# Squared key lengths from the diagonal of the key scores, on VectorE, in a gated delta rule

## The chip, the cores and the metric

One core of a Trainium2 chip runs the whole program in one launch. The time is device microseconds of one execution; the profiled execution also has a trace of every instruction.

## The reference

One layer of a hybrid block on 256 tokens of width 2048, batch 1, all in float32. A modulated RMSNorm of `x` goes through one wide input projection. Its columns feed two branches: a bidirectional mLSTM (4 heads) and a bidirectional gated delta rule (16 heads of width 128). Both are projected back, merged by gates and projected once more; a SwiGLU feed-forward part (5632 wide) and a last RMSNorm follow. The change is inside the gated delta rule, in the lengths of keys and queries:

```python
def l2_normalize(a):
    return a * lax.rsqrt(jnp.sum(a * a, axis=-1, keepdims=True) + EPS)

q_b = l2_normalize(heads(b_q, B_HEADS, B_DK)) * (B_DK ** -0.5)
k_b = l2_normalize(heads(b_k, B_HEADS, B_DK))
...
a_mat = jnp.eye(CHUNK) + betac[..., :, None] * jnp.einsum('nbhid,nbhjd->nbhij', kc, kc) * decay_strict
t_mat = lax.linalg.triangular_solve(a_mat, eye, left_side=True, lower=True, unit_diagonal=True)
u = jnp.einsum('nbhij,nbhje->nbhie', t_mat, betac[..., None] * vc)
```

For each token and head one needs the squared length of its key and of its query. The products of all keys with all keys, which the rule needs anyway, hold the squared key lengths on their diagonal.

## The kernel before

Large products run on TensorE in a split form: a float32 weight tile is copied to a high part `wh` by ScalarE (lines 178 and 209), VectorE subtracts it to get the low part `wl` (lines 180 and 211), and three matmuls a tile (lines 183 to 185, or 230 to 232) give the product. `wh` and `wl` have three buffers each. The jobs that do this (`fjob`, `tjob`) are generators; they are the filler between the steps of the delta rule, and `pump` adds a row product of the modulation (line 123, on VectorE) from time to time.

The delta rule runs head by head through `gdn_phase1`. Step one of a head makes the decay masks `dec` by scans on VectorE, splits keys and queries `kq` (128 x 2 x 256, width by kind by token) into `kqh` and `kql`, squares `kq` on ScalarE (`sqkq`, line 602), transposes the values into the PSUM tile `vps` (line 605), and multiplies each of the four 128-token blocks of squares by a column of ones (line 607). These four one-column products leave the squared lengths of keys and queries in columns 256 to 259 of `vps`, one token to a partition. Step two takes their roots (line 615, Sqrt on ScalarE), the reciprocals `r4`, the squared reciprocal of the key length, and from it and `beta` the factors `sig` and `nsg` (lines 616 to 622, four small VectorE instructions), and scales the values into `vv` (line 625, ScalarE, which frees `vps`). Then for each of the two 128-token blocks `t` three matmuls give the scores `ks` of its keys with all keys and queries (lines 636 to 638), and VectorE makes five masked products of them: `mi` and `mb` from the diagonal block (lines 643 and 644, with `nsg` as a factor for each partition), `gg` and `at` from the rest (lines 646 to 652). A 32x32 transpose (line 653) fills the second half of `mi`, GpSimd's queue stores blocks of it (`inst_d`, line 659), and ScalarE copies corners of `mi` and `mb` to `cc`.

After four heads, `gdn_invert` solves the small triangles on VectorE, and `gdn_phase2` runs two heads at a time through short products (`p`, `pa`, `pb`, `pc`, `po`, `px`) while `stream` feeds in the projections (`b_job`, a convolution and Silu on the way) and `gdn_phase1` of the heads of the next group. `vps`, `ks` and all tiles of the second phase come from one PSUM pool of four banks, `g_ps`.

The order of instructions on an engine is not the order of the text: a planner lists them by simulated readiness, with the text's order as priority, and only instructions wrapped in `order(...)` stay behind their predecessor on that engine. None of the lines that the change touches is wrapped.

Of the kernel before, what the change touches and what calls it, by code (L numbers as in the profile page):

```python
# [9 lines left out]
F32 = mybir.dt.float32  # L10
F32R = mybir.dt.float32r
AF = mybir.ActivationFunctionType
# [3 lines left out]
P = 128  # L16
T = 256
# [35 lines left out]
def hybrid_block(ctx: ExitStack, tc: tile.TileContext, xr, nfr, crow, pk_d, cst_d, ada2, ada4, win0, winb, wint, wba, wbb, wo, wgu, wd, out, dbg=None):  # L53
# [529 lines left out]
    def gdn_phase1(h):  # L583
# [16 lines left out]
        V.tensor_tensor(kl, kq, kh.bitcast(F32), ALU.subtract)  # L600
        sq = fr.tile([P, 2, T], F32, tag="sqkq", bufs=1, name=f"sqkq{h}")
        S.activation(sq, kq, AF.Square)
        vps = gps(f"vps{h}")
        for t in range(2):
            PE.transpose(vps[:, t * P : (t + 1) * P], vf[:, t * P : (t + 1) * P], ident)
        for c in range(4):
            PE.matmul(
                vps[:, 256 + c : 257 + c], sq[:, c // 2, (c % 2) * P : (c % 2 + 1) * P], ones1, start=True, stop=True
            )
        yield  # L610
# [3 lines left out]
        nn = fr.tile([P, 8], F32, tag="nn", bufs=2, name=f"nn{h}")  # L614
        S.activation(nn[:, 0:4], vps[:, 256:260], AF.Sqrt, bias=epsc)
        V.reciprocal(r4, nn[:, 0:4])
        V.tensor_tensor(nn[:, 4:6], r4[:, 0:2], r4[:, 0:2], ALU.mult)
        beta = bT[:, :, h::16]
        sg3, ns3 = (a.rearrange("p (t d) -> p t d", t=2) for a in (sig, nsg))
        rk2 = nn[:, 4:6].unsqueeze(2).broadcast_to([P, 2, 2])  # L620
        V.tensor_tensor(sg3, beta, rk2, ALU.mult)
        V.tensor_scalar(nsg, sig, -1.0, None, ALU.mult)
        vv = bk.tile([P, 2, P], F32, tag="vv", bufs=NB, name=f"vv{h}")
        for t in range(2):
            S.activation(vv[:, t], vps[:, t * P : (t + 1) * P], AF.Copy, scale=nn[:, t : t + 1])


# [3 lines left out]
        at = bk.tile([P, 2, 384], F32, tag="at", bufs=NB, name=f"at{h}")  # L631
        for t in range(2):
            ks = gps(f"ks{h}_{t}")
            c = slice(t * P, (t + 1) * P)
            mh, ml_ = (a.rearrange("p j t -> p t j") for a in (kh, kl))
            PE.matmul(ks, kh[:, 0, c], mh, start=True, stop=False)
            PE.matmul(ks, kh[:, 0, c], ml_, start=False, stop=False)
            PE.matmul(ks, kl[:, 0, c], mh, start=False, stop=True)
            kk, qk = (a for a in (ks.rearrange("p (t j) -> p j t", j=2)[:, j] for j in range(2)))
            dg = kk[:, t * P : (t + 1) * P]  # L640
            fdiag = dec[:, 0, 0:P] if t == 0 else dec[:, 0, 256:384]
            bdiag = dec[:, 1, 256:384] if t == 0 else dec[:, 1, P:256]
            V.scalar_tensor_tensor(mi[:, t], dg, ns3[:, t, 0:1], fdiag, ALU.mult, ALU.mult)
            V.scalar_tensor_tensor(mb[:, t], dg, ns3[:, t, 1:2], bdiag, ALU.mult, ALU.mult)
            if t == 0:
                V.tensor_tensor(gg[:, 0], kk[:, P:], dec[:, 0, P:256], ALU.mult)
                V.tensor_tensor(at[:, 0, 0:256], qk, dec[:, 0, 0:256], ALU.mult)
                V.tensor_tensor(at[:, 1, 256:384], qk[:, 0:P], dec[:, 1, 256:384], ALU.mult)
            else:
                V.tensor_tensor(gg[:, 1], kk[:, 0:P], dec[:, 1, 0:P], ALU.mult)  # L650
                V.tensor_tensor(at[:, 0, 256:384], qk[:, P:], dec[:, 0, 256:384], ALU.mult)
                V.tensor_tensor(at[:, 1, 0:256], qk, dec[:, 1, 0:256], ALU.mult)
        V.transpose(mi[:, 2:4].rearrange("p t c -> p (t c)"), mb.rearrange("p t c -> p (t c)"))
        g, hl_ = divmod(h, GRP)
# [902 lines left out]
```

## Time and profile before

| | us |
|---|---|
| Runs | 1971.29, 1970.10, 1968.26 (median 1970.1) |
| Profiled execution | 1969.12 |
| its span | 1966.6 |
| TensorE busy | 1925.2 |
| VectorE busy | 1406.0 |
| ScalarE busy | 1028.7 |
| GpSimd busy | 116.5 |

A trace row has a start and a duration in microseconds, the engine, the line of the kernel, the operation, and the tile written and read. A row of a group has, after the bar, the busy time in all and the mean of one in nanoseconds, then the engine's idle time just before these instructions and what ended it. A row of waits has the total in microseconds, the number of waits and the longest. PE is TensorE, PEld its weight load, DVE VectorE, ACT ScalarE, POOL GpSimd. A row with `x2` or more merges neighbours.

### The profile page before, as it was taken

To read this page: it belongs to the slowest core of one execution; us is meant where nothing else is said; L and a number is where in the kernel's file an instruction comes from. 1 tells how busy PE (TensorE), PEld (TensorE's weight loads), DVE (VectorE), ACT (ScalarE), POOL (GpSimd) and SP (SyncE) were. 2 spreads that over 40 slices of the span, in tenths; PEclk is the share of its full clock that TensorE was granted. 3 is DMA by queue.
4 is the path that set the end of the run, shared out by engine and by line. 5 is a ranking of instruction groups with operands and counts; after the bars stand their busy time and mean duration, and the time that the engine had idled before them with its cause. 6 is when DMAs were issued, how large, how long until landed. Compare 5 with 4: busy or idle time off the path is not lost. (4 is left out here: it accounts for less than half of the span.)

```text
span 1966.6 us, 27097 instructions
## 1 busy us (share of the span) xinstructions
PE 1925.2 (98%) x10418; PEld 1701.1 (86%) x10418; DVE 1406.0 (71%) x2067; ACT 1028.7 (52%) x1553; POOL 116.5 (6%) x211
## 2 busy tenths in 40 slices
PE   8999999999999999999999999999999999999998
PEld 6888889998999899888787888888888888888886
DVE  6779886887888799866577988765666665555554
ACT  3137656765776587564544444644444444444444
POOL 0001210111011101110100000200000000000000
PEclk9999999999999999999999999999999999999999
DMA  9986677667576766586686998566676665565554
GB/s 400 420 351 224 187 248 254 216 222 236 213 237 194 237 221 230 193 286 230 235 310 250 348 356 325 176 252 238 248 261 237 238 244 202 193 214 202 205 201 142
DMA packets 78962, 485.64 MB, mean 247 GB/s; under 512 B 10585, under 2 KB 15969, under 8 KB 24433
## 3 DMA queue, kind: packets, MB, share of 16 engines
q1 hardware_dynamic: 63216, 450.69, 63.0%
q0 software_dynamic: 8160, 17.88, 4.3%
q10 hardware_dynamic: 7458, 15.36, 2.1%
q8 instruction: 81, 1.33, 0.3%
q14 instruction: 47, 0.39, 0.1%
HBM read 467.07 MB, written 16.82 MB: 246 GB/s over the span
## 5 line engine op out<-in xcount | busy, mean ns | idle before, releaser
L211 DVE TENSOR_TENSOR wl_d<-raw_d,wh_d 128x1024 fp32r<-128x1024 f32 x88 | 107.6, 1224 | 105.9 <-ACT wh_d L209 105.9
L211 DVE TENSOR_TENSOR wl_up<-raw_up,wh_up 128x1024 fp32r<-128x1024 f32 x88 | 107.7, 1224 | 100.2 <-ACT wh_up L209 100.1
L211 DVE TENSOR_TENSOR wl_gt<-raw_gt,wh_gt 128x1024 fp32r<-128x1024 f32 x88 | 108.1, 1228 | 80.3 <-ACT wh_gt L209 80.3
L183 PE MATMUL acc_b<-hh,wh_b 128*128 128x256 f32 x576 | 161.8, 281 | 0.0
L209 ACT ACTIVATE wh_d<-raw_d 128x1024 fp32r<-128x1024 f32 x88 | 92.9, 1056 | 126.4 <-PE acc_d L231 117.6
L185 PE MATMUL acc_b<-hh,wl_b 128*128 128x256 f32 x576 | 158.7, 276 | 0.1
L184 PE MATMUL acc_b<-hl,wh_b 128*128 128x256 f32 x576 | 158.3, 275 | 0.0
L209 ACT ACTIVATE wh_gt<-raw_gt 128x1024 fp32r<-128x1024 f32 x88 | 92.9, 1055 | 118.6 <-PE acc_gt L231 71.1
L209 ACT ACTIVATE wh_up<-raw_up 128x1024 fp32r<-128x1024 f32 x88 | 92.7, 1055 | 108.1 <-PE acc_up L231 77.1
L123 DVE SCALAR_TENSOR_TENSOR ada<-ada,crow 128x2048 f32<-128x2048 f32 x64 | 146.1, 2283 | 0.0
L230 PE MATMUL acc_gt<-wh_gt,hfh 128*128 128x512 f32 x352 | 135.4, 385 | 0.6 <-ACT hfh L1344 0.6
L231 PE MATMUL acc_gt<-wh_gt,hfl 128*128 128x512 f32 x352 | 135.1, 384 | 0.0
L232 PE MATMUL acc_gt<-wl_gt,hfh 128*128 128x512 f32 x352 | 134.2, 381 | 0.0
L230 PE MATMUL acc_up<-wh_up,hfh 128*128 128x512 f32 x352 | 133.4, 379 | 0.0
L231 PE MATMUL acc_up<-wh_up,hfl 128*128 128x512 f32 x352 | 133.4, 379 | 0.0
L232 PE MATMUL acc_up<-wl_up,hfh 128*128 128x512 f32 x352 | 133.4, 379 | 0.0
L230 PE MATMUL acc_d<-wh_d,ffh 128*128 128x512 f32 x344 | 130.5, 379 | 0.0
L231 PE MATMUL acc_d<-wh_d,ffl 128*128 128x512 f32 x344 | 130.5, 379 | 0.0
L232 PE MATMUL acc_d<-wl_d,ffh 128*128 128x512 f32 x344 | 130.4, 379 | 0.0
L557 PE MATMUL first<-x,raw 128*128 128x256 f32 x512 | 114.5, 382 | 6.8 <-ACT x L551 6.3
L557 PEld LDWEIGHTS first<-x,raw 128*128 128x128 f32 x512 | 96.0, 190 | 25.3 <-ACT x L551 11.9
L184 PEld LDWEIGHTS acc_b<-hl,wh_b 128*128 128x128 f32 x576 | 110.6, 192 | 0.1
(383 smaller groups left out, 5257.5 us busy)
## 6 DMA issues: line engine op xcount, KB each, us to landing
ada<-ada SPq DMA_DIRECT2D x64, 1024.0 KB, 6.1
raw_gt<-wgu SPq DMA_DIRECT2D x44, 1024.0 KB, 4.9
raw_up<-wgu SPq DMA_DIRECT2D x44, 1024.0 KB, 4.9
raw_d<-wd SPq DMA_DIRECT2D x44, 1024.0 KB, 4.8
raw_b<-winb SPq DMA_DIRECT2D x36, 1024.0 KB, 5.6
ra<-ada SPq DMA_DIRECT2D x32, 1025.0 KB, 15.7
raw<-win SPq DMA_DIRECT2D x16, 1024.0 KB, 14.6
raw_z<-wint SPq DMA_DIRECT2D x16, 1024.0 KB, 4.9
```

The costliest lines, as they stand in the source:

```text
L123: order(V.scalar_tensor_tensor(raw, raw, 1.0, row_c[:, :D], ALU.mult, ALU.mult, accum_out=mod[:, c : c + 1]))
L183: PE.matmul(o, wh[:, k], woven(hh[:, kk]), start=kk == 0, stop=False)
L184: PE.matmul(o, wh[:, k], woven(hl[:, kk]), start=False, stop=False)
L185: PE.matmul(o, wl[:, k], woven(hh[:, kk]), start=False, stop=kk == KB - 1)
L209: order(S.activation(wh, raws[u][:, k0 : k0 + 2], AF.Copy), early)
L211: order(V.tensor_tensor(wl, raws[u][:, k0 : k0 + 2], wh.bitcast(F32), ALU.subtract), early)
L230: order(PE.matmul(ps[t], xh[:, kk, c], woven(wh[:, k]), start=kk == 0, stop=False), early and steps > 1)
L231: PE.matmul(ps[t], xl[:, kk, c], woven(wh[:, k]), start=False, stop=False)
L232: PE.matmul(ps[t], xh[:, kk, c], woven(wl[:, k]), start=False, stop=kk == last)
L557: PE.matmul(first[o], raw[:, o], x[:, b], start=b == 0 and o % 2 == 0, stop=b == KB - 1 and o % 2 == 1)
```

## The change

The squares are taken of the queries alone, and two one-column products in place of four give the squared query lengths (columns 258 and 259 of `vps`). Both score tiles of a head are computed first (`scores`), and from each one VectorE instruction multiplies the diagonal block by the identity and sums along the row (`accum_out`): the squared key lengths, in `nn`. It writes its full product into the second half of `mi`, which the transpose overwrites later. The keys' and the queries' roots are two Sqrt instructions. The masks of the off-diagonal parts (`masked`) come next, then the reciprocals and small factors, then the diagonal masks, and with them the scaled values `vv`.

```diff
@@ -598,38 +598,28 @@
         kl = fr.tile([P, 2, T], F32R, tag="kql", bufs=1, name=f"kql{h}")
         S.activation(kh, kq, AF.Copy)
         V.tensor_tensor(kl, kq, kh.bitcast(F32), ALU.subtract)
-        sq = fr.tile([P, 2, T], F32, tag="sqkq", bufs=1, name=f"sqkq{h}")
-        S.activation(sq, kq, AF.Square)
+        sq = fr.tile([P, T], F32, tag="sqkq", bufs=1, name=f"sqkq{h}")
+        S.activation(sq, kq[:, 1], AF.Square)
         vps = gps(f"vps{h}")
         for t in range(2):
             PE.transpose(vps[:, t * P : (t + 1) * P], vf[:, t * P : (t + 1) * P], ident)
-        for c in range(4):
-            PE.matmul(
-                vps[:, 256 + c : 257 + c], sq[:, c // 2, (c % 2) * P : (c % 2 + 1) * P], ones1, start=True, stop=True
-            )
+        for t in range(2):
+            PE.matmul(vps[:, 258 + t : 259 + t], sq[:, t * P : (t + 1) * P], ones1, start=True, stop=True)
         yield
         settle()
         sm = bk.tile([P, 12], F32, tag="sm", bufs=NB + 1, name=f"sm{h}")
         r4, sig, nsg = sm[:, 0:4], sm[:, 4:8], sm[:, 8:12]
         nn = fr.tile([P, 8], F32, tag="nn", bufs=2, name=f"nn{h}")
-        S.activation(nn[:, 0:4], vps[:, 256:260], AF.Sqrt, bias=epsc)
-        V.reciprocal(r4, nn[:, 0:4])
-        V.tensor_tensor(nn[:, 4:6], r4[:, 0:2], r4[:, 0:2], ALU.mult)
         beta = bT[:, :, h::16]
         sg3, ns3 = (a.rearrange("p (t d) -> p t d", t=2) for a in (sig, nsg))
         rk2 = nn[:, 4:6].unsqueeze(2).broadcast_to([P, 2, 2])
-        V.tensor_tensor(sg3, beta, rk2, ALU.mult)
-        V.tensor_scalar(nsg, sig, -1.0, None, ALU.mult)
         vv = bk.tile([P, 2, P], F32, tag="vv", bufs=NB, name=f"vv{h}")
-        for t in range(2):
-            S.activation(vv[:, t], vps[:, t * P : (t + 1) * P], AF.Copy, scale=nn[:, t : t + 1])
-
 
         mi = fr.tile([P, 4, P], F32, tag="mi", bufs=1, name=f"mi{h}")
         mb = fr.tile([P, 2, P], F32, tag="mb", bufs=1, name=f"mb{h}")
         gg = bk.tile([P, 2, P], F32, tag="gg", bufs=NB, name=f"gg{h}")
         at = bk.tile([P, 2, 384], F32, tag="at", bufs=NB, name=f"at{h}")
-        for t in range(2):
+        def scores(t):
             ks = gps(f"ks{h}_{t}")
             c = slice(t * P, (t + 1) * P)
             mh, ml_ = (a.rearrange("p j t -> p t j") for a in (kh, kl))
@@ -637,11 +627,12 @@
             PE.matmul(ks, kh[:, 0, c], ml_, start=False, stop=False)
             PE.matmul(ks, kl[:, 0, c], mh, start=False, stop=True)
             kk, qk = (a for a in (ks.rearrange("p (t j) -> p j t", j=2)[:, j] for j in range(2)))
-            dg = kk[:, t * P : (t + 1) * P]
-            fdiag = dec[:, 0, 0:P] if t == 0 else dec[:, 0, 256:384]
-            bdiag = dec[:, 1, 256:384] if t == 0 else dec[:, 1, P:256]
-            V.scalar_tensor_tensor(mi[:, t], dg, ns3[:, t, 0:1], fdiag, ALU.mult, ALU.mult)
-            V.scalar_tensor_tensor(mb[:, t], dg, ns3[:, t, 1:2], bdiag, ALU.mult, ALU.mult)
+            V.scalar_tensor_tensor(
+                mi[:, 2 + t], kk[:, c], 1.0, ident, ALU.mult, ALU.mult, accum_out=nn[:, 6 + t : 7 + t]
+            )
+            return kk, qk, kk[:, c]
+
+        def masked(t, kk, qk, dg):
             if t == 0:
                 V.tensor_tensor(gg[:, 0], kk[:, P:], dec[:, 0, P:256], ALU.mult)
                 V.tensor_tensor(at[:, 0, 0:256], qk, dec[:, 0, 0:256], ALU.mult)
@@ -650,6 +641,22 @@
                 V.tensor_tensor(gg[:, 1], kk[:, 0:P], dec[:, 1, 0:P], ALU.mult)
                 V.tensor_tensor(at[:, 0, 256:384], qk[:, P:], dec[:, 0, 256:384], ALU.mult)
                 V.tensor_tensor(at[:, 1, 0:256], qk, dec[:, 1, 0:256], ALU.mult)
+
+        both = [scores(t) for t in range(2)]
+        S.activation(nn[:, 0:2], nn[:, 6:8], AF.Sqrt, bias=epsc)
+        S.activation(nn[:, 2:4], vps[:, 258:260], AF.Sqrt, bias=epsc)
+        masked(0, *both[0])
+        masked(1, *both[1])
+        V.reciprocal(r4, nn[:, 0:4])
+        V.tensor_tensor(nn[:, 4:6], r4[:, 0:2], r4[:, 0:2], ALU.mult)
+        V.tensor_tensor(sg3, beta, rk2, ALU.mult)
+        V.tensor_scalar(nsg, sig, -1.0, None, ALU.mult)
+        for t, (kk, qk, dg) in enumerate(both):
+            fdiag = dec[:, 0, 0:P] if t == 0 else dec[:, 0, 256:384]
+            bdiag = dec[:, 1, 256:384] if t == 0 else dec[:, 1, P:256]
+            V.scalar_tensor_tensor(mi[:, t], dg, ns3[:, t, 0:1], fdiag, ALU.mult, ALU.mult)
+            V.scalar_tensor_tensor(mb[:, t], dg, ns3[:, t, 1:2], bdiag, ALU.mult, ALU.mult)
+            S.activation(vv[:, t], vps[:, t * P : (t + 1) * P], AF.Copy, scale=nn[:, t : t + 1])
         V.transpose(mi[:, 2:4].rearrange("p t c -> p (t c)"), mb.rearrange("p t c -> p (t c)"))
         g, hl_ = divmod(h, GRP)
         if g not in uus:
```

## The prediction

> **What bounds the kernel now.** I read the page first, for the engines and the granted clock.
>
> ```profile
> PE 1925.2 (98%) x10418; PEld 1701.1 (86%) x10418; DVE 1406.0 (71%) x2067; ACT 1028.7 (52%) x1553; POOL 116.5 (6%) x211
> PEclk9999999999999999999999999999999999999999
> ```
>
> TensorE is busy all the time at the full clock, so an instruction taken off it is worth its slot in TensorE's stream, and whatever makes TensorE wait is worth that wait. The change touches only `gdn_phase1`, whose 16 heads run between 190 and 800 us. So I asked for busy time by stretch, and then for what TensorE waited for inside that stretch.
>
> ```profile
> core 0: us, PE busy (x) PEld busy (x) DVE busy (x) ACT busy (x) POOL busy (x), PEclk, DMA share, GB/s
> 0.00:190.00 190.00, 177.51 (x779) 146.90 (x780) 140.56 (x192) 70.69 (x118) 6.42 (x19) 1.00 0.89 350
> 190.00:800.00 610.00, 602.50 (x4112) 561.54 (x4111) 511.19 (x1018) 411.06 (x756) 77.12 (x149) 1.00 0.68 225
> 800.00:1966.60 1166.60, 1145.16 (x5531) 992.61 (x5529) 754.22 (x858) 546.95 (x681) 32.95 (x45) 0.99 0.67 242
> ```
>
> ```profile
> PE acc_mb L232 <- DVE wl_mb L211: 1.9, 2, 1.4
> PE p L791 <- DVE pt L780: 1.5, 1, 1.5
> PE acc_o L232 <- DVE wl_o L211: 1.4, 2, 1.0
> PE p L766 <- DVE pt L758: 1.2, 1, 1.2
> ...
> PE pb L815 <- DVE r L816: 0.7, 3, 0.2
> ```
>
> In these 610 us TensorE is idle for 7.5 us, and 6.7 us of that (the five rows) is waiting for VectorE. VectorE is busy for 511 us, 84%, and has 99 us free. VectorE is the engine that gets new work. So the question is whether TensorE's saving outweighs what a fuller VectorE, and a new round trip between VectorE and ScalarE, make TensorE wait.
>
> ScalarE and VectorE feed TensorE with split weights (`wh`, `wl`), three buffers deep. Whether they run ahead is seen in what ScalarE waits for:
>
> ```profile
> ACT wh_b L178 <- PE acc_b L184: 30.5, 26, 2.6
> ACT wh_o L209 <- PE acc_o L231: 19.8, 13, 2.2
> ACT wh_mb L209 <- PE acc_mb L231: 16.8, 11, 2.5
> ```
>
> These three alone are 67 us in 50 waits in which ScalarE had a tile ready to split and no free buffer. The feed is then full, and a delay of VectorE is absorbed by up to two tiles.
>
> **The change, part by part.**
>
> *TensorE, removed.* Four one-column products a head become two.
>
> ```profile
> L607 PE MATMUL vps<-ones,sqkq 128*128 128x1 f32 x128 | 15.3, 241 | 0.0
> 788.07 0.95 PE L607 MATMUL vps<-ones,sqkq 128*128 128x1 f32 x8
> 788.88 0.36 PE L183 MATMUL acc_a<-hh,wh_a 128*128 128x256 f32 x1
> ```
>
> 128 instructions over 16 heads are 8 a head, two for each product. Their 241 ns overlap; what counts is the pitch: eight of them start at 788.07 and the next matmul at 788.88, so (788.88 - 788.07) / 8 = 0.101 us each. 64 fall away: 64 x 0.101 = 6.5 us. With TensorE at 98.8% of this stretch, all of it is on the path. The score products, transposes and everything else of TensorE stay as many as they were.
>
> *VectorE, added.* Two multiply-and-sum instructions a head over 128x128, one input in PSUM, and the read of the accumulator that follows each.
>
> ```profile
> 795.18 0.35 DVE L643 SCALAR_TENSOR_TENSOR mi<-ks,sm,dec 128x128 f32<-128x128 f32 x1 [1.12 <-PE ks L638]
> 795.44 0.34 DVE L644 SCALAR_TENSOR_TENSOR mb<-ks,sm,dec 128x128 f32<-128x128 f32 x1
> L123 DVE DVE_READ_ACCUMULATOR ada<-ada,crow 128x1 f32 x18 | 1.5, 81 | 0.0
> ```
>
> The same shape from the same PSUM tile takes 0.26 us from start to start, and an accumulator read takes 0.08: 0.34 us, and 32 x 0.34 = 10.9 us. This goes into the 99 us that VectorE has free. If the free time were evenly spread, TensorE's 6.7 us of waits for VectorE would grow by 10.9 / 99, that is by 0.7 us. If nothing covered it, it would cost 10.9 us. I take 0.7, because the feed is mostly full (above).
>
> *ScalarE.* The square covers 256 columns in place of 512, and one small Sqrt becomes two.
>
> ```profile
> L602 ACT ACTIVATE sqkq<-kq 128x512 f32<-128x512 f32 x16 | 10.0, 623 | 0.2 <-PE vps L607 0.2
> L337 ACT ACTIVATE vf<-cv 128x256 f32<-128x256 f32 x16 | 6.7, 418 | 14.5 <-DVE cv L334 14.1
> L615 ACT ACTIVATE nn<-vps,epsc 128x4 f32<-128x4 f32 x16 | 4.0, 262 | 0.2
> ```
>
> A 256-column activation takes 418 ns, so the square saves 0.2 us and the second Sqrt costs 0.26 us: +0.06 us a head, 1 us over 16 heads, on an engine that is busy for 411 of 610 us. I cost it at nothing. What is not nothing is where the keys' Sqrt now stands. Before, both lengths came from `vps`, were rooted at once, and the four small instructions behind them were done before the scores existed. After, the keys' Sqrt needs the scores, about 6 us later, and between the two places other activations change ScalarE's function table:
>
> ```profile
> 404.82 1.28 ACT L615 ACT_TABLE_LOAD   x1
> 406.12 0.26 ACT L615 ACTIVATE nn<-vps,epsc 128x4 f32<-128x4 f32 x1
> 408.62 1.28 ACT L337 ACT_TABLE_LOAD   x1
> 415.84 1.06 ACT L209 ACTIVATE wh_mb<-raw_mb 128x1024 fp32r<-128x1024 f32 x1
> ```
>
> At this head Sqrt's table is loaded at 404.82 and Silu's at 408.62, and the masks of the scores come only from 412 us on (rows further down). The keys' Sqrt would have to load its table once more and Silu once more after it: 2 x 1.28 us. ScalarE's timeline shows such a Silu between Sqrt and scores for heads 4, 6, 8, 10, 12, 14 and for the pair 0 and 1: 8 heads. For the other eight nothing but a copy or a Sqrt lies between. That is about 16 loads, 21 us of ScalarE, inside its free 199 us.
>
> *The new wait.* VectorE's reciprocal now waits for ScalarE's Sqrt, which waits for VectorE's sums. Behind the reciprocal on VectorE stand the diagonal masks, the 32x32 transpose and then `wl` splits and convolutions; behind the Sqrt on ScalarE stand `wh` splits and Silus. What covers the round trip are the six off-diagonal masks, written ahead of the reciprocal:
>
> ```profile
> 412.63 0.28 DVE L646 TENSOR_TENSOR gg<-ks,dec 128x128 f32<-128x128 f32 x1
> 413.36 0.34 DVE L643 SCALAR_TENSOR_TENSOR mi<-ks,sm,dec 128x128 f32<-128x128 f32 x1
> ...
> 416.54 2.32 DVE L211 TENSOR_TENSOR wl_mb<-raw_mb,wh_mb 128x1024 fp32r<-128x1024 f32 x2
> 419.24 0.38 PE L232 MATMUL acc_mb<-wl_mb,hh 128*128 128x512 f32 x1
> ```
>
> Three of them run from 412.63 to 413.36, 0.73 us; six cover 1.46 us. The Sqrt needs 0.26 us without a table load and 1.30 + 0.26 = 1.56 us with one (404.82 to 406.12 is 1.30). So VectorE stands still for 0 or 0.1 us when ScalarE is free, and up to 1.06 us more when a `wh` split has just begun. At this head VectorE reaches `wl_mb` at 416.54, has the first of two tiles at about 416.54 + 2.32 / 2 = 417.70, and TensorE reads it at 419.24: a lead of 1.54 us. After the change VectorE comes to it later by the sums (0.68), by the four small instructions that move here (from the row below and its successor about 0.2 each, 0.8) and by the stall (0.1 to 1.1): 1.6 to 2.6 us. TensorE would then wait 0.1 to 1.1 us.
>
> ```profile
> 406.42 0.18 DVE L616 RECIPROCAL sm<-nn 128x4 f32<-128x4 f32 x1
> 406.63 0.16 DVE L617 TENSOR_TENSOR nn<-sm 128x2 f32<-128x2 f32 x1
> 413.62 0.47 DVE L334 SCALAR_TENSOR_TENSOR cv<-pad,pk,cv 128x256 f32<-128x256 f32 x1
> ```
>
> I take the low end, 0.1 us, at the 8 heads with a table change, 0.8 us in all. The last row is why: the order on an engine is not that of the text but a planner's, which puts ready work into gaps (here a convolution step between two masks of one score tile), so it will put a ready `wl` split ahead of the reciprocal rather than behind it.
>
> The Trainium skill, page "ScalarE: Activation LUTs", section "What ACT_TABLE_LOAD costs", speaks against the change: a table switch is given as 1.28 us of load and 1.38 us of drain, 2.66 us. The trace has the 1.28, but its next activation starts 1.30 us after the load's start, so no drain shows here; by the page's figure the stall at those 8 heads would be 2.66 + 0.26 - 1.46 = 1.46 us each, an estimate, and the sum would come out at 1976 us.
>
> *Buffers and queues.* `vps` is now held until `vv` is made at the end. Around 412 us that makes `vps`, two score tiles and the `pc` of the second phase: four tiles for the four banks of that pool, so nothing waits so long as the next tile comes later.
>
> ```profile
> 415.23 0.39 PE L803 MATMUL pc<-r,UL 128*128 128x128 f32 x2
> 421.39 0.38 PE L825 MATMUL po<-z,at 128*128 128x128 f32 x2
> POOL inst_d L659 <- DVE mi L653: 369.0, 15, 56.2
> DVE utmp L700 <- DMA uu<-inst_d: 3.2, 2, 1.9
> ```
>
> The next, `po`, comes at 421.39; before, masks and transpose were done at 416.54, after at about 419. Nothing, then; if that cover were gone, TensorE's stream would stand still for the rest of the round trip, and I let that be part of the slower case. The transposed mask leaves 2 to 3 us later, and so do GpSimd's four transfers of it. GpSimd waits for that mask anyway (369 us). Only the last head of a group of four is awaited, by the inversion, where VectorE waits 3.2 us in all; TensorE has several tiles of filler queued there. I cost it at nothing.
>
> *Sum.* -6.5 + 0.7 + 0.8 = -5.0 us. The profiled execution took 1969.1 us, of which the span is 1966.6; the median of the runs is 1970.1, 1.0 above. So 1964.1 against the profiled execution and 1965.1 against the median; I forecast 1965.1.
>
> **Rivals.**
>
> *The lead is gone at the eight heads with a table change.* Each costs TensorE about 0.8 us, inside the 0.1 to 1.1 worked out above; 8 x 0.8 = 6.4 eats the 6.5. Time 1970.0. For it: at the head shown the lead is only 1.54 us. Against: the planner, and the full feed.
>
> *The round trip costs at every head (slower).* The keys' Sqrt stands behind a `wh` split each time, VectorE stands in its queue behind the reciprocal, the held banks push the second phase back, and TensorE pays 1.1 us at 16 heads: 17.6 - 6.5 = +11.1, time 1981.2. It decides from 6.5 / 16 = 0.41 us a head; above 0.65 us a head the kernel is measurably slower. For it: the planner's durations are not the chip's, and a wrong guess of the moment at which a Sqrt is ready turns into an in-order wait on two engines; TensorE's idle time of 7.5 us in 610 leaves no reserve. Against: ScalarE's 67 us and more of waiting for free buffers. The drain that the Trainium skill gives would push this way.
>
> *Nothing is freed.* The two passes left cost what four did, because a pass's place is set by the weight load before it or by the switch from and to full-width products. Time about 1970. Against: the eight passes above follow at an even 0.1 us and take 0.81 us between two full-width streams.
>
> **How the numbers follow.** A measurement of this kernel can tell about 0.2%, 3.9 us, from no change. I give the forecast 0.50, of which 0.03 falls inside 0.2%; the eight heads 0.12; nothing freed 0.05; the slower rival 0.33. So faster 0.47, same 0.20, slower 0.33. The forecast's own range is 1961.7 (all 6.5 us, and the 1.9 us of the largest group of waits gone by another order) to 1966.2. The whole range goes up to the slower rival at 14 heads, 14 x 1.1 - 6.5 = 8.9, 1979, and down to 1962; that leaves out about 0.12 above and 0.05 below.
>
> **What would show it right or wrong.** In the profile after: 64 one-column matmuls in place of 128, with the same pitch; 32 more accumulator reads on VectorE, and VectorE busy for some 522 us in the stretch; Sqrt loads up from 10 to about 18. The forecast is right if TensorE's waits for VectorE and ScalarE in the stretch grow from 6.7 us to about 8. It is wrong if waits of the reciprocal for the Sqrt, or of `wl` for `wh`, come to more than some 10 us and TensorE's waits for `wl` grow with them, or if TensorE waits for a score bank that `vv` or a mask still holds.

## The result and the profile after

The kernel became slower. After the change the runs have a median of 1989.46 us (6 runs, 1983.85 to 1992.86), beside 1969.18 us of the kernel before on the same chip: a ratio of 1.0098, 95% interval 1.0082 to 1.0115. That is some 19 us; a gain of 5 had been forecast, and the range ended at 1979. The profiled execution took 1983.85 us (before 1969.12), with a span of 1981.7 us (before 1966.6). It is the shortest of the six, so its trace explains 15 us; the rest lies in executions without a trace. Part of that rest is the clock: TensorE's mean granted clock was 0.994 in the profiled execution and 0.988 and 0.989 in the two longest, which is some 10 us.

The same line of the page, the same stretch of the busy times, and the groups of instructions that the change touches:

```profile
PE 1924.5 (97%) x10354; PEld 1694.1 (85%) x10354; DVE 1412.3 (71%) x2131; ACT 1048.7 (53%) x1585; POOL 116.9 (6%) x211
```

```profile
190.00:800.00 610.00, 591.49 (x3966) 546.13 (x3965) 507.04 (x1049) 423.50 (x770) 75.34 (x145) 0.99 0.66 221
```

```profile
L337 ACT ACT_TABLE_LOAD x23 | 29.5, 1283 | 0.4
...
L647 ACT ACT_TABLE_LOAD x11 | 14.1, 1283 | 0.2
...
L630 DVE SCALAR_TENSOR_TENSOR mi<-ks,cst 128x128 f32<-128x128 f32 x32 | 9.0, 287 | 19.0 <-PE ks L628 12.0 <-DMA inst_d<-mi 6.9
L646 ACT ACT_TABLE_LOAD x7 | 9.0, 1283 | 0.1
...
L607 PE MATMUL vps<-ones,sqkq 128*128 128x1 f32 x64 | 8.1, 230 | 0.0
```

The change does what it says: 64 one-column passes, 32 sums. TensorE is idle for 57.2 us of the span (1981.7 - 1924.5) where it was idle for 41.4, and for 18.5 us of the 610 where it was 7.5. What TensorE waits for between 190 and 1000 us is still mostly VectorE. These views are the waits in that stretch (total, number, longest): a row of TensorE in the kernel before, TensorE in the kernel after, a row of VectorE in the kernel before, VectorE in the kernel after:

```profile
PE acc_mb L232 <- DVE wl_mb L211: 2.3, 3, 1.4
```

```profile
PE acc_mb L232 <- DVE wl_mb L211: 8.2, 3, 3.9
PE p L798 <- DVE pt L787: 4.4, 4, 1.9
...
PE acc_v L232 <- DVE wl_v L211: 3.9, 3, 2.2
```

```profile
DVE utmp L700 <- DMA uu<-inst_d: 5.1, 3, 1.9
```

```profile
DVE utmp L707 <- DMA uu<-inst_d: 17.0, 4, 6.2
...
DVE mi L630 <- DMA inst_d<-mi: 6.9, 2, 3.5
DVE cg L728 <- DMA bc<-mal_d: 6.3, 1, 6.3
DVE cg L728 <- DMA cg<-inv_d: 4.9, 2, 3.3
```

The four rows of the kernel after are 35.1 us in which VectorE stands in front of a transfer. In the kernel before, the same stretch has no wait of `mi` for `inst_d`, and 5.1 us of `utmp` and 7.5 of `cg`. `utmp` is the first product of the inversion and waits for the transposed masks of four heads, stored and read back by GpSimd's queue. `cg` is the transpose of the inverses read back. Whatever stands behind such an instruction on VectorE, the `wl` splits above all, stands too. One such place, the start of the first inversion, in the timeline of the kernel before and then of the kernel after:

```profile
258.53 0.16 DVE L700 TENSOR_TENSOR utmp<-uu 64x30 f32<-64x30 f32 x1
```

```profile
273.93 0.19 DVE L707 TENSOR_TENSOR utmp<-uu 64x30 f32<-64x30 f32 x1 [6.18 <-DMA uu<-inst_d]
...
274.52 1.21 DVE L211 TENSOR_TENSOR wl_mb<-raw_mb,wh_mb 128x1024 fp32r<-128x1024 f32 x1
...
275.79 0.48 PE L232 MATMUL acc_mb<-wl_mb,hh 128*128 128x512 f32 x1 [3.87 <-DVE wl_mb L211]
...
276.32 0.38 PE L231 MATMUL acc_mb<-wh_mb,hl 128*128 128x512 f32 x1
...
276.54 0.44 PE L232 MATMUL acc_mb<-wl_mb,hh 128*128 128x512 f32 x1
...
276.77 0.63 PE L230 MATMUL acc_mb<-wh_mb,hh 128*128 128x512 f32 x1
...
277.19 0.63 PE L231 MATMUL acc_mb<-wh_mb,hl 128*128 128x512 f32 x1
```

VectorE stands for 6.18 us, `wl_mb` comes late, and TensorE stands for 3.87. The last four rows show a second price: the same matmul, started every 0.22 us at first, is started every 0.42 us from 276.77 on. The busy time by stretch has it as the granted clock, the number after POOL's bracket:

```profile
220.00:230.00 10.00, 7.75 (x29) 6.18 (x28) 10.00 (x22) 6.42 (x14) 3.47 (x7) 0.83 0.61 143
...
270.00:280.00 10.00, 6.13 (x21) 4.79 (x20) 5.70 (x18) 1.91 (x2) 1.29 (x3) 0.84 0.52 118
```

In the trace's clock record these are stretches of 3.41 us at half clock, each worth 1.7 us. Between 190 and 1000 us there are two before (at 924 and 968 us) and four after (226, 277, 656 and 983), each starting within 1.2 us of the moment at which TensorE came back from a gap of 1.9 to 4.0 us.

So there are three things to add for a kernel: TensorE's idle time, the time lost at reduced clock (length times one minus the clock) and the slots of the one-column passes, 0.101 us each. Against the profile before (span 1966.6, idle 41.5, lost at reduced clock 7.7):

| kernel | change of span | idle | clock | slots | sum of the three | clock, mean of all runs |
|---|---|---|---|---|---|---|
| after | +15.1 | +15.7 | +3.4 | -6.5 | +12.6 | +4.9 |
| e1 two products alone | +5.5 | +7.7 | +7.0 | -6.5 | +8.2 | +4.2 |
| e14 the same, one tile more | -8.6 | -1.1 | +2.0 | -6.5 | -5.6 | +2.2 |
| e2 sums alone | +8.2 | +2.1 | +6.7 | 0 | +8.8 | +1.2 |
| e17 the same, one tile more | +12.9 | +4.4 | +8.6 | 0 | +13.0 | +4.3 |
| e13 other order | +16.8 | +14.6 | +7.1 | -6.5 | +15.2 | +4.8 |
| e6 short tail | +13.4 | +8.7 | +8.6 | -6.5 | +10.8 | +3.3 |
| e12 short tail, one tile more | +3.3 | +0.1 | +7.1 | -6.5 | +0.7 | +1.9 |
| e8 before, more filler | +18.5 | +5.9 | +16.9 | 0 | +22.8 | +12.4 |

The sum meets the span within 4.3 us. The table is used below: it says in which of the three a kernel differs. All but its last column are of one profiled execution each, which can lie some us from the median of its kernel (e6's is its slowest, e14's its fastest). The clock above all differs between executions of one kernel: the kernel before lost 7.7 us in its profiled execution, but 11 us on average in the runs beside the experiments, at granted clocks of 0.992 to 0.997. So the last column compares the means of all runs, from the clock recorded for each (for the kernel after, against those 11 us).

Where along the way the time is lost shows in TensorE's progress, read at the moments when ScalarE empties the same accumulator in both kernels. The kernel after is 1.2 us ahead at 209 us, 3.9 behind at 232, 7.1 at 256, 12.3 at 297, and then about level, mostly at 11 to 14, until 795; 3 us more come after 800. All of the loss but those 3 us falls in the first four heads. (The slots saved go into that difference, so after 297 something else still takes about as much as they give.)

### The profile page after: what moved, and what is told of

Its sections match the earlier page's. It is cut to its first block, busy times and chain, and to the rows that moved or that the text cites. A ratio compares the mean times of both kernels' runs of the same rounds, so it can differ in the third digit from the quotient of the medians.

```text
span 1981.7 us, 27026 instructions
## 1 busy us (share of the span) xinstructions
PE 1924.5 (97%) x10354; PEld 1694.1 (85%) x10354; DVE 1412.3 (71%) x2131; ACT 1048.7 (53%) x1585; POOL 116.9 (6%) x211
## 6 DMA issues: line engine op xcount, KB each, us to landing
raw<-win SPq DMA_DIRECT2D x16, 1024.0 KB, 14.5
```

## The experiments

All were timed beside the kernel before on the same chip. The texts on record were written before each run, with the theories as they then stood. Their letters mean: A, the chain through the single mask tile `mi` in the first group; B, a VectorE that is too full; C, the round trip to the Sqrt; D, VectorE standing in front of instructions that GpSimd's transfers feed; E, any new order of the instructions shifts the engines against the transfers, by amounts without relation to the edit. Differences in us are the ratio's, times 1969 us.

**The price of a slot: three or six products a head.** The kernel before with another number of one-column products.

```diff
-        for c in range(4):            # before
+        for c in range(6):            # e10: the keys' two products twice
+        for c, n in ((0, 2), (2, 1), (3, 1)):   # e9: one product fills both key columns
```

> The kernel before with three one-column products a head in place of four: the first block's key lengths stand in for the second block's, so the numbers are not the reference's; nothing else changes. If TensorE's slots alone set the time: 3.2 us faster. Theory E (a new plan moves VectorE's and TensorE's places against the transfers, and what that costs has no relation to the size of the edit): any sign, between 6 us faster and 8 us slower, with the difference made in steps at the inversions and the reads of the inverses.

> The kernel before with six one-column products a head in place of four: the keys' two are made twice, the second time into unused columns. If TensorE's slots alone set the time: 3.2 us for 32 products of two passes at 0.101 us more, that is 6.5 us slower. Theory E: any sign, and off from +6.5 by several us, with the difference made in steps at the inversions and the reads of the inverses.

e9 (the second block's keys get the first block's lengths): 1966.57 us, ratio 0.9977 (0.9967 to 0.9988), 4.5 us less for two fewer passes a head; the slots are 3.2. e10: 1976.47 us, 1.0038 (1.0025 to 1.005), 7.5 us more; the slots are 6.5. Both intervals (2.4 to 6.5 us less, 4.9 to 9.8 more) hold the price of 0.1 us a pass, and removing a product does pay.

**The two halves of the change alone.** e1 is the kernel before with the queries' two products only, whose lengths stand in for the keys'; e2 is the kernel before plus the two sums, unused, in a tile of their own.

```diff
# e1
-        S.activation(sq, kq, AF.Square)
+        S.activation(sq, kq[:, 1], AF.Square)
-        for c in range(4): PE.matmul(vps[:, 256 + c : 257 + c], ...)
+        for t in range(2): PE.matmul(vps[:, 258 + t : 259 + t], ...)
# e2
+            V.scalar_tensor_tensor(jk[:, t], dg, 1.0, ident, ALU.mult, ALU.mult, accum_out=nn[:, 6 + t : 7 + t])
```

> The kernel before with the removal alone: two one-column products a head instead of four, half the square, and no sums on VectorE; the queries' lengths stand in for the keys' too, so the numbers of this kernel are not the reference's, and the order of the steps is that of before. Theory A (the loss comes from the chain through the single mask tile mi in the first group, not from TensorE): 5 to 7 us faster than before, 64 x 0.101 = 6.5. Rival 'nothing is freed': no difference, within 2 us. Rival 'any new plan costs TensorE some waits': slower than -3 us, with new waits for wl of some us.

> The kernel before with the addition alone: the two sums a head are made on VectorE, into a scratch tile of their own, and not used. Theory A: VectorE has room, so no more than 3 us slower than before. Rival B (VectorE is too full): 10 us or more slower, with the waits of TensorE for wl grown as in the changed kernel, from 7.7 to some 20 us.

e1: 1974.37 us, 1.0023 (1.0011 to 1.0035); e2: 1976.14 us, 1.0033 (1.002 to 1.0046). Even the half that only takes work away made the kernel slower. Its progress is 2.6 us ahead until 482 us and then loses in three steps, at 485 to 500, 665 to 688 and 845 to 868, where VectorE stands at `cg`. In the waits of VectorE, before and then e1:

```profile
DVE cg L721 <- DMA cg<-inv_d: 3.9, 2, 2.8
DVE cg L721 <- DMA bc<-mal_d: 3.6, 1, 3.6
```

```profile
DVE cg L719 <- DMA cg<-inv_d: 11.1, 2, 6.3
DVE cg L719 <- DMA bc<-mal_d: 5.9, 1, 5.9
```

VectorE doesn't come to this read sooner after the store of the inverses; the inverses come back later. Their store by GpSimd and the transpose that reads them back, in the third group, before and then in e1:

```profile
660.66 2.30 POOL L692 DMA_DIRECT2D inv_d<-uu  x4 [17.47 <-DVE uu L706]
674.02 0.71 DVE L721 STREAM_TRANSPOSE cg<-cg 128x512 f32<-128x512 f32 x1 [2.76 <-DMA cg<-inv_d]
```

```profile
658.35 2.29 POOL L690 DMA_DIRECT2D inv_d<-uu  x4 [17.48 <-DVE uu L704]
675.25 0.71 DVE L719 STREAM_TRANSPOSE cg<-cg 128x512 f32<-128x512 f32 x1 [6.30 <-DMA cg<-inv_d]
```

VectorE is ready for the read 10.6 us after the store in both (674.02 - 2.76 - 660.66 and 675.25 - 6.30 - 658.35). From store to transpose it takes 13.4 us before and 16.9 in e1. In the last three groups VectorE is ready after 10.6 to 11.1 us in both kernels, and the transpose starts after 12.0, 13.4 and 14.5 us before and after 15.7, 16.9 and 17.0 in e1. Why the transfers take 2.5 to 3.7 us longer is open. Whether more cover helps was tested: e14 gives e1 one more filler tile there in the last three groups, e15 gives it to the kernel before, e17 to e2.

```diff
-        fill(7 if g else 8)
+        fill(8)
```

> The kernel before with two products a head instead of four (key lengths replaced by the queries'), as in the run of that name, and one more filler tile before the read of the inverses in the last three groups. Theory (that run's loss of about 5 us against its nominal 6.5 us of gain sits in three waits of VectorE for the read of the inverses, 4.9 to 6.3 us each, that TensorE feels): the waits shrink to 1 to 4 us and the time falls to 1966 to 1970 us. Rival (the loss is spread, a filler tile only moves work away from the stage's end): 1973 to 1977 us, as without it.

> The kernel before with the one more filler tile before the read of the inverses, nothing else. If the tile is worth something only where VectorE stands long at the read (4 us and more), the time is 1968 to 1972 us, no change, since these waits are 1.1, 2.8 and 3.6 us here. If the tile is a gain of its own, 1962 to 1966 us, and the 7 us that it brought to the short tail say nothing about the change.

> The kernel before with the two sums on VectorE, unused, in a tile of their own (four products stay), and the one more filler tile before the read of the inverses. Without the tile the sums cost 6.5 us. Theory VectorE load (the sums cost by themselves, because VectorE's work comes later and TensorE waits for it a little everywhere): 1973 to 1977 us still. Rival (here too the cost is the missing cover at the awaited transfers): 1967 to 1971 us, nothing left, and then the 7 us between the short tail with the tile and the two products alone with the tile must lie in the other part of the tail, not in the sums.

e14: 1962.37 us, 0.9968 (0.9956 to 0.9979). That is 6.3 us below the kernel before, which is the 6.5 us of slots, whole. Its waits at `cg`:

```profile
DVE cg L719 <- DMA cg<-inv_d: 3.1, 2, 1.6
DVE cg L719 <- DMA bc<-mal_d: 0.6, 1, 0.6
```

e15: 1969.64 us, 1.0003 (0.9995 to 1.0012): the tile is no gain of its own. So the loss of e1 is shown to lie at that transfer, which the tile covers (VectorE is ready after 12.5 to 13.6 us in e14; the transfers take 13.1 to 15.2). e17: 1981.03 us, 1.0059 (1.0045 to 1.0072): here the tile doesn't help, and the sums cost more with it than without. In the profiled executions of the two kernels with the sums, the loss at reduced clock grows more than the idle time (6.7 and 8.6 us); over all runs it grows by 1.2 and 4.3 us only, so most of what the sums cost isn't the clock. Each has one long wait at the inversion, 5.75 us at 632.6 and 5.85 us at 638.8, beside 1.8 us in e14. It comes from GpSimd's queue, where the read-back waits for the four stores of the last head; e2 and then e14, in GpSimd's timeline:

```profile
620.68 2.18 POOL L661 DMA_DIRECT2D inst_d<-mi  x4 [13.57 <-DVE wl_z L211]
627.32 0.51 POOL L668 DMA_DIRECT2D uu<-inst_d  x1 [4.46 <-DMA inst_d<-mi]
```

```profile
615.94 2.18 POOL L657 DMA_DIRECT2D inst_d<-mi  x4 [12.91 <-DVE wl_z L211]
619.93 0.52 POOL L664 DMA_DIRECT2D uu<-inst_d  x1 [1.81 <-DMA inst_d<-mi]
```

GpSimd waits 2.7 us longer for the stores in e2. The four stores take some 6.2 us from the first issue to the last landing there in e6, e12, e13, e16, e17 and e18 too, and 3.4 in the kernel before (3.9 in the kernel after). Why they do at that head is open.

**The tile that the sums write (e3, e4).** The sums leave their full product in the second half of `mi`, which has one buffer, so they wait until the head before has been stored (the 6.9 us above). e3 gives the sums a tile of their own, e4 gives `mi` two buffers.

```diff
-                mi[:, 2 + t], kk[:, c], 1.0, ident, ...
+                jk[:, t], kk[:, c], 1.0, ident, ...              # e3
-        mi = fr.tile([P, 4, P], F32, tag="mi", bufs=1, ...)
+        mi = fr.tile([P, 4, P], F32, tag="mi", bufs=2, ...)      # e4
```

> The changed kernel, but the sums write their unused product into a tile of their own and not into the second half of mi, which GpSimd's transfers of the head before still read. Theory A: VectorE's two waits of 3.5 us of that instruction for those transfers go, the diagonal masks still wait for them; 4 to 9 us faster than the changed kernel, that is 11 to 16 us slower than before. Rival B (VectorE's load, or the Sqrt's round trip): as slow as the changed kernel, 17 to 23 us over before.

> The changed kernel with two buffers for mi in place of one. No head then waits for the transfers of the head before. Theory A: the heads of the first group follow each other some 4 to 5 us sooner, the inversion of the first group starts 10 us sooner, and 10 to 15 us come back: 5 to 10 us slower than before. Rival B: as slow as the changed kernel, 17 to 23 us over before.

e3: 1990.46 us, 1.0103 (1.0087 to 1.0119); e4: 1990.56 us, 1.0107 (1.009 to 1.0123). The theory fell. The waits for `inst_d` are gone, and VectorE stands at the next things that came late instead; in the waits of e4:

```profile
DVE cg L728 <- DMA cg<-inv_d: 16.8, 3, 6.1
DVE utmp L707 <- DMA uu<-inst_d: 16.3, 4, 5.9
DVE dec L590 <- DMA al<-alpha_d: 6.6, 2, 4.5
```

**Why the transposed mask is late (e11, e13, e6).** From the last score product of a head to the transpose of its masks it takes 1.9 to 3.5 us in heads 4 to 15 of the kernel before, and 5.2 to 9.8 us after. In heads 0 to 3 it takes 2.8, 8.0, 2.6 and 6.7 us before, and 8.6, 12.9, 7.8 and 15.1 after. VectorE's timeline at head 2 of the kernel after:

```profile
241.09 0.08 DVE L630 DVE_READ_ACCUMULATOR mi<-ks,cst 128x1 f32 x1
...
242.46 0.41 DVE L643 TENSOR_TENSOR at<-ks,dec 128x256 f32<-128x256 f32 x1
242.79 0.17 DVE L650 RECIPROCAL sm<-nn 128x4 f32<-128x4 f32 x1
...
245.35 0.34 DVE L658 SCALAR_TENSOR_TENSOR mb<-ks,sm,dec 128x128 f32<-128x128 f32 x1
245.61 1.22 DVE L211 TENSOR_TENSOR wl_v<-raw_v,wh_v 128x1024 fp32r<-128x1024 f32 x1
...
248.56 0.42 DVE L660 STREAM_TRANSPOSE mi<-mb 128x256 f32<-128x256 f32 x1
```

The sums are in at 241.2, the six masks hold the reciprocal until 242.8, a split stands between it and the factors, and the diagonal masks end at 245.7; a split and the next head's scans stand before the transpose. Two suspects: the Sqrt round trip and the order. e11 takes the factors as 1 / (sum + eps) on VectorE, without the round trip, in the same order. e13 keeps the round trip and moves the six masks behind the transpose. e6 does both and gives the sums a tile of their own.

```diff
# e11 and e6
-        V.reciprocal(r4, nn[:, 0:4])       # moves further down
-        V.tensor_tensor(nn[:, 4:6], r4[:, 0:2], r4[:, 0:2], ALU.mult)
+        V.tensor_scalar(nn[:, 4:6], nn[:, 6:8], EPS, None, ALU.add)
+        V.reciprocal(nn[:, 4:6], nn[:, 4:6])
# e13 and e6
-        masked(0, *both[0]); masked(1, *both[1])
         ... reciprocal, factors, diagonal masks ...
         V.transpose(mi[:, 2:4]..., mb...)
+        masked(0, *both[0]); masked(1, *both[1])
```

> The changed kernel with one difference: the factors of the diagonal masks are made on VectorE as 1 / (sum + eps) and no longer wait for ScalarE's Sqrt; the masks keep their order and the sums still go through mi. If the round trip is the reason for the longer way from the scores to the transposed mask: the way falls from 5 to 10 us to 4 to 6 us, the first group loses less than 4 us in place of 13.5, and the kernel is 4 to 12 us over before. If the order of the masks or the sums' tile is the reason: 14 to 21 us over before.

> The kernel after with one move: reciprocal, factors, diagonal masks and the 32x32 transpose stand ahead of the six off-diagonal masks; the square-root round trip, the scratch in mi and everything else stay. Theory order (the transposed mask leaves late because it stands behind six masks and both score tiles): from the scores to the transpose 2 to 8 us a head, as with the short tail, the first group's loss of 12 us gone, time 1977 to 1982 us. Rival (the round trip counts as soon as nothing covers it): VectorE waits for the Sqrt at most heads, 0.3 to 2.8 us each, 10 to 25 us in all, scores to transpose 5 to 10 us as in the kernel after, time 1985 to 1995 us.

> The changed kernel with a short way from the scores to the transposed mask: the factors are made on VectorE as 1 / (sum + eps), without the Sqrt, the diagonal masks come before the off-diagonal ones, and the sums have a tile of their own. Same work on TensorE, the Sqrt stays for the values alone. Theory D with a longer way as the reason: the transposed mask leaves within 3 to 5 us of the scores as before, VectorE's waits for transfers fall to 12 to 20 us, and 8 to 18 us come back: 2 to 12 us over before. Rival 'any new plan costs': 15 us or more over before, with waits at other places.

| | us | ratio (interval) | scores to transpose, heads 0 to 3 | us behind at 297 | at 635 |
|---|---|---|---|---|---|
| after | 1989.46 | 1.0098 (1.0082 to 1.0115) | 8.6, 12.9, 7.8, 15.1 | +12.3 | +11.0 |
| e11 | 1993.34 | 1.0115 (1.0101 to 1.0129) | 8.6, 12.5, 7.9, 15.3 | +13.0 | +12.4 |
| e13 | 1986.7 | 1.0097 (1.0082 to 1.0112) | 4.4, 7.2, 4.0, 7.3 | +1.1 | +12.7 |
| e6 | 1978.29 | 1.0047 (1.0033 to 1.006) | 4.1, 5.9, 3.7, 7.0 | +0.3 | +0.2 |

e11: in this order, the round trip isn't what makes the mask late. e13: the order is. With the six masks behind the transpose the first group's loss is gone, which settles where those 12 us came from. But e13's time is no better, because it loses about as much later, in heads where e6 doesn't. Its largest gaps there are 3.09 us at 430.8 and 3.07 at 614.9, both at a late `wl`; ahead of that, VectorE stands at a step of the convolution that waits for ScalarE:

```profile
418.58 2.34 DVE L211 TENSOR_TENSOR wl_mb<-raw_mb,wh_mb 128x1024 fp32r<-128x1024 f32 x2
423.26 0.49 DVE L334 SCALAR_TENSOR_TENSOR cv<-pad,pk,cv 128x256 f32<-128x256 f32 x1 [2.33 <-ACT cv L332]
423.66 2.28 DVE L123 SCALAR_TENSOR_TENSOR ada<-ada,crow 128x2048 f32<-128x2048 f32 x1
```

The rival's signature for e13, 10 to 25 us of waits for the Sqrt, isn't there: they are 3.5 us in six. So its time came near the rival's number without the rival's waits. In e6 TensorE waits 0.25 us at each of the two places. ScalarE's timelines differ there, at both places, in the six copies of the mask's corners to `cc`: at the first one they are made at 414.1 to 415.8 in e6, ahead of Silu's table load, and at 420.1 to 421.8 in e13, behind it and right ahead of the convolution step (422.7) for which VectorE stands. The diagonal masks that they copy end 3.8 us after the sums in e13 and 2.0 us in e6. That these later masks make ScalarE's next work late is read from the traces and not tested. Between e13 and e6 lie the round trip and the sums' tile; which of the two decides wasn't tried apart.

**What is left of the short tail (e12, e16, e18).** e6 still loses 4 to 5 us around 680 and again around 865, where VectorE stands at `cg` (and 4 more between 893 and 931). e12 gives it the one more filler tile of e14; e16 gives it to e13; e18 saves e12 one VectorE instruction a head, the constant being added inside the sum (its expectation says that it enters 128 times; it enters once, as the identity is zero elsewhere).

> The kernel with the short way, and one more tile of filler ahead of the read of the inverses in the last three groups. The three waits of VectorE for those reads, 4.4 to 5.9 us, fall by about 2.6 each; theory D gives 3 to 6 us back: 3 to 6 us over before. Theory E, or a lack of filler at the end of the stage: 8 us or more over before.

> The kernel after with the move of the diagonal masks and the transpose ahead of the six masks, and one more filler tile before the read of the inverses; the square-root round trip stays. Theory order plus waits at the read: 1970 to 1975 us, the same as before within 0.2%, as with the short tail without the round trip. Rival (the round trip counts once uncovered): 1980 to 1990 us.

> The short tail with the one more filler tile (1971.1 us, the same as before) with one VectorE instruction less a head: the small constant is added inside the multiply-and-sum (128 of them in each sum, no longer once a token) and the reciprocal reads the sums directly. 16 x 0.2 = 3.2 us less of VectorE, and the diagonal masks start 0.2 us earlier. If the path runs through VectorE's tail at every head: 1967 to 1969 us. If TensorE doesn't feel 0.2 us a head: 1970 to 1972 us.

e12: 1971.08 us, 1.0006 (0.9997 to 1.0014). e16: 1986.28 us, 1.0092 (1.0078 to 1.0106). e18: 1969.72 us, 1.0004 (0.9995 to 1.0013). VectorE's waits at `cg` in e6, and in e12:

```profile
DVE cg L730 <- DMA cg<-inv_d: 10.2, 2, 5.8
DVE cg L730 <- DMA mkq<-kq_d: 5.9, 1, 5.9
```

```profile
DVE utmp L709 <- issue: 6.1, 1, 6.1
DVE cg L730 <- DMA cg<-inv_d: 5.3, 2, 4.0
DVE cg L730 <- DMA bc<-mal_d: 1.1, 1, 1.1
```

So 18 of the 19 us are had back by another order, factors without the round trip, a tile for the sums and one tile of filler; they weren't the price of the work that the change adds. None of the versions with the whole computation is measurably below the kernel before: between e14 and e12, which have the same passes and the same filler, lie 7.5 us, and what differs is VectorE's sums and tail. They use up the 6.5 us of slots. The first row of e12 is a stand of 6.1 us before the third inversion for which the profile names no releaser; in the trace the read-back of the masks lands 0.1 us before it ends, and e2 and e17 stand there too, with the transfer named.

**More filler everywhere (e5, e7, e8).** Two or three tiles more before both awaited transfers: in the kernel after, in e6 and in the kernel before.

```diff
-        fill(4 if g else 6)
+        fill(6 if g else 9)
-        fill(7 if g else 8)
+        fill(9 if g else 10)
```

> The changed kernel with two (at the first group three) more tiles of filler ahead of each inversion, and two more ahead of each read of the inverses, so that VectorE comes to these two instructions after their transfers have landed. Theory D (VectorE stands in its queue in front of instructions that GpSimd's transfers feed, and the weight splits behind it come late): VectorE's waits for transfers fall from 35 us to under 15, TensorE's waits for VectorE from 25 to about 15, and 6 to 12 us come back: 8 to 14 us over before. Rival C (the Sqrt's round trip and its table loads cost by themselves) and rival B (VectorE's load): no change, 17 to 23 us over before.

> The two edits of the runs before in one: short way and more filler ahead of the inversion and of the read of the inverses. Theory D: both act, VectorE's waits for transfers under 10 us, TensorE's waits for VectorE at or below the 10.6 us of before, and the 6.5 us of removed products begin to show: between 5 us faster and 4 us slower than before. Rival 'any new plan costs': 8 us or more over before.

> The kernel before with the same additional filler at the two places, nothing else. Theory D: VectorE's 12.5 us of waits for transfers go, TensorE's idle time falls by 2 to 5 us, and the kernel is 2 to 5 us faster. Rival 'any new plan costs': 3 to 8 us slower than before.

e5: 2001.27 us, 1.0156 (1.014 to 1.0171); e7: 1993.32 us, 1.0122 (1.0106 to 1.0137); e8: 1985.48 us, 1.008 (1.0066 to 1.0095). VectorE's waits for transfers shrink (from 35.1 to 17.9 us in e5, from 12.6 to 4.5 in e8), yet all three are slower. The filler is a fixed stock: what is used here is missing at the stage's end. In e8 most of the cost is the clock, +16.9 us in the profiled execution and +12.4 over all runs, which I read as the short products at the end being left without full-width ones among them. The test was too coarse for what it should show; one tile in three places (e14, e12) showed it.

## Why the prediction was wrong, point by point

The sum was to be -5.0 us and is +19.3. By the experiments it is made of -6.3 for the products (e14), +7.5 for VectorE's sums and tail (e14 to e12) and +18.1 for the order, the round trip, the sums' tile and the missing tile of filler (e12 to the kernel after).

- *TensorE, removed, -6.5 us.* Right: e14 gives 6.3 us, e9 and e10 agree. But it is only had if the awaited transfer is covered; in e1, where the transfer took longer, it turned into a loss of 4.5 us. The prediction's rival that nothing is freed fell with it.
- *VectorE, added, +0.7 us.* Mis-sized. The sums alone cost 6.5 us (e2), 11.6 with other cover (e17), though they are only 9.0 us of busy time in a stretch with 99 us free. The formula spread TensorE's waits over free time. It left out that VectorE works in order and stands before transfers, and that a gap can be followed by half clock. How the 6.5 us divide between these isn't shown.
- *ScalarE.* The count was right (16 more loads: 15 to 23 at Silu's line, 10 to 18 at Sqrt's). The trace of after again shows no drain behind a load (at 58 of its 66 loads the next activation starts 1.29 us after the load's start): neither kernel has the 1.38 us that the Trainium skill, page "ScalarE: Activation LUTs", section "What ACT_TABLE_LOAD costs", adds. It is so in e13 too, where a load at 411.94 is followed by its Sqrt at 413.23:

```profile
411.94 1.28 ACT L646 ACT_TABLE_LOAD   x1
413.23 0.29 ACT L646 ACTIVATE nn<-nn,epsc 128x2 f32<-128x2 f32 x1
```

- *The new wait, +0.8 us.* Right in what it looked at: VectorE's reciprocal hardly waits, since the six masks cover the Sqrt. It looked at the wrong instruction. The cover itself is what makes the masks late that are stored.
- *Buffers and queues, 0.* This step failed. "The transposed mask leaves 2 to 3 us later ... I cost it at nothing." Counted from the scores it leaves 5.8, 4.9, 5.2 and 8.4 us later in heads 0 to 3, and 3 to 7 us later in heads 4 to 15. And it isn't only the last head of a group that is awaited: `mi` has one buffer, so the next head's sums wait for the store; with that wait gone (e4), its scans wait for `al`, which stands behind the masks in GpSimd's queue. The first inversion began at 273.93; before the change, at 258.53. The filler that was named as cover can't hide VectorE's stand, because the filler itself needs VectorE's `wl`. TensorE lost 12.3 us there (e13 and e6 lose 1.1 and 0.3). TensorE's only wait for a PSUM bank in the stretch is 0.2 us, of a score product at 204.8 for `vv`; that part held for its idle time. But the scores of head 3 now end 5.5 us after those of head 2 (246.25 and 240.75), and before 2.7 us after: their second block starts at 245.44, just after the last mask of head 2's first block (245.18). That would fit a bank still held by a mask, while TensorE does other work; no run tests it.
- *The rivals.* The slower one, "the round trip costs at every head", had the sign and, at 1981.2 us for a profiled 1983.85 and a median of 1989.46, part of the size, with a chance of 0.33. That was luck, because its mechanism was wrong: without the round trip (e11) the time didn't fall, and the loss is in four heads, not in sixteen.
- *The range* took its upper end from a price per head. A loss that comes as a few steps of 3 to 5 us, some with 1.7 us of half clock, had no place in it.

## What to carry to other kernels

When work moves into an in-order engine, follow not the instruction that newly waits but every transfer that starts later because of it, through its queue, to the instruction on that same engine that awaits it: the filler meant to hide the wait may need that engine too. Put what is stored and read back ahead of what only the next stage reads. And a saving on the busiest engine can be hidden by a transfer that takes longer in the new order: try it together with one more tile of cover, in just those places, before it is judged.

## What the runs showed of the hardware

TensorE's granted clock fell to one half for 3.41 us after single gaps, in a stage in which it was 97% busy: after a gap of 2.25 us at 224.3, of 1.90 at 654.8, of 3.87 at 275.8. A gap of 1.90 us at 475.1 had no such stretch. So a gap of about 2 us cost 2 or 3.7 us. The traces show what decides. In each of the 20 the stretches start at whole multiples of 3.413 us from one another; in the kernel after at 225.53, 276.73, 655.61 and 983.29, which is 15, 126 and 222 steps from the first. Cut at these steps, the gap that ended at 654.8 lies in one window (652.20 to 655.61), and the one that ended at 475.1 in two, with 1.5 and 0.4 us. Between 190 and 1000 us no window in which TensorE stood idle for more than 1.98 us was followed by one at full clock, in any trace; with 1.18 to 1.98 us both happened. The Trainium skill, page "TensorE: Matmul & The Clock Gate", section "HAM oscillation — how this bites in real kernels", puts the limit at idle gaps above some 3.4 us; here shorter ones were enough. Its Part 1 gives a free-running window of that length; the traces agree, with 3.413 us.

The four small stores of a mask, 16 KB each, took a median of 1.7 us to land in e14 around 618 us and 3.2 us in e6 at the same head, with weight loads of 1 MB under way in both.
